# Chunked attention on one core: the softmax scaling moved from GpSimd to ScalarE, TensorE held to the lanes' order, one entry of the planner's table lowered

## The chip, the core and the metric

One core of a Trainium2 chip runs the whole kernel. Times are device microseconds (us) of one execution; the time before is the median of three runs. Engines are named as in the profile: PE is TensorE (PEld its weight loads), DVE is VectorE, ACT is ScalarE, POOL is GpSimd, SP is SyncE, which issues most DMAs. Each engine takes its instructions in the order in which they stand in its own queue; between engines, semaphores make one wait for another.

## The reference

A trunk of two layers over 1024 positions of width 1024, float32. Layer 0 mixes with two recurrent head groups, layer 1 with chunked softmax attention; each layer then has an MLP of width 4096 and a gated embedding. The change touches only the attention:

```python
CHUNK, C_HEADS, C_HEAD_DIM, C_WINDOW_CHUNKS, C_MAX_REL = 64, 16, 64, 8, 256

def chunk_band_attention(h, w_qkv, q_g, k_g, rel_bias):
    qkv = (h @ w_qkv).reshape(bsz, seq, 3, C_HEADS, C_HEAD_DIM)
    q = rmsnorm(qkv[:, :, 0], q_g) * (C_HEAD_DIM ** -0.5)
    k = rmsnorm(qkv[:, :, 1], k_g)
    v = qkv[:, :, 2]
    ...
    def one_chunk(c):          # a chunk of 64 queries against its own and the previous 8 chunks
        ...
        s = jnp.einsum('bqhd,bkhd->bhqk', q_c, k_b).astype(jnp.float32) + bias
        s = jnp.where(valid, s, -jnp.inf)
        prob = jax.nn.softmax(s, -1).astype(v.dtype)
        return jnp.einsum('bhqk,bkhd->bqhd', prob, v_b)
```

## The kernel before

All large products run on PE in three passes (high times high, high times low, low times high), with each operand split into a rounded part and a rest. Layer 0 and the tails of both layers (output product, MLP, gate) fill most of the time; the attention of layer 1 is a stretch of some 590 us in the middle of the profile.

**Work of the attention.** There are 16 steps: 8 pairs of heads (`pr`) times two halves of the sequence (`hf`), each of 512 queries. `attn_in` makes q, k and v of a step: dense matmuls into the bank `dps` (24 of 128x384 for 128 positions), then ACT copies q and k out (`qk`, L1699), ACT and DVE the two parts of v (`vs`, L1703 and L1704), and POOL squares and DVE sums and normalises q and k (L1711 to L1715). `attn_norm` transposes q and k on PE (`dps` from `qk`) and splits them (`F`, `Ql`, L1737 to L1740).

**A job** is `attn_block`: one step, one head, 256 queries; 64 jobs in all. For each of its two blocks of 128 queries:

- near scores into the PSUM tile `sn` (up to 384 keys, two banks in turn) and, from the fourth block of the sequence on, far scores into `sf` (up to 256 keys, one bank for all jobs);
- DVE adds the bias to the near scores and takes their maximum (L1795, into the SBUF tile `pb`), masks a corner of the far ones (L1802), takes their maximum (L1803) and forms the negative of the larger (L1804, or L1807 where there are no far ones);
- ACT takes the exp of the far and of the near scores with their sums (L1805, L1808; each has a second row that reads the sum);
- DVE adds the two sums (L1810) and takes the reciprocal (L1811);
- POOL multiplies the block's probabilities, 128 to 640 columns, by it (L1812).

Then PE transposes the probabilities of both blocks, 128x128 at a time, into `pt` (two banks), ACT copies each bank into `ptile` (L317) and DVE writes the rest of the split (L318), and PE multiplies with v into `po` (one bank for the two jobs of a head). After the second job of a head ACT and DVE move the output out (L1853, L1854).

**Order.** The order in which the program writes its instructions comes from `run` (L123): generators, called lanes, yield the name of a waiting time, and the planner's clock `self.now` advances by a price for each matmul (L151 to L165). A lane goes on when the clock has passed its yield by the table's entry in `LAT` (L37); other lanes fill the time. Two attention lanes take the jobs in turn; the other two lanes are `attn_norms` and `attn_ins`, and the latter also does the embedding's product and the first part of the output product (`dps` from `act` and `wq`, 128x512). In a job, `attn_block0` is the time after each block's scores, `attn_block1` the additional time before the transposes, `attn_block2` that after each bank of transposes, `attn_block3` that before the products with v.

On top of it the framework's own scheduler (the context is opened with a simulated timeline) orders each engine's queue anew when the program is closed, by its own estimate of when an instruction can start. In the kernel before it does so for all engines, PE among them.

Of the kernel before, what the change touches and what calls it, by code (L numbers as in the profile page):

```python
# [11 lines left out]
AF = mybir.ActivationFunctionType  # L12
ALU = mybir.AluOpType
# [4 lines left out]
P = 128  # L18
# [60 lines left out]
    "gdn_back4": 1.83,  # L79
    "attn_norm0": 0.24,  # L80
    "attn_block0": 0.97,
    "attn_block1": 4.45,
    "attn_block2": 0.43,
    "attn_block3": 0.94,
    "qk": 11.25,
# [19 lines left out]
class Trunk:  # L105
# [1470 lines left out]
    def layer1_in(self):  # L1576
        nc, tc, a = self.nc, self.tc, self.a
        with ExitStack() as es:
            self.psm = es.enter_context(self.pool("psml1", space=PSUM))
            wp = self.wp = es.enter_context(self.pool("l1a", 2))  # L1580
            self.wr = es.enter_context(self.pool("l1wr", 2))
            self.w1 = es.enter_context(self.pool("l1w1"))
            l1 = es.enter_context(self.pool("l1", 2))
            self.sm = es.enter_context(self.pool("sml1", 2))
            self.yd = [[self.dr.tile([P, HB], F32, tag=f"yd{k}{hf}", name="yd") for hf in range(2)] for k in range(NK)]
            rbl = l1.tile([P, 16], F32, tag="rbl", name="rbl", bufs=1)
            nc.sync.dma_start(out=rbl, in_=a["rb_last"].rearrange("(o c) -> o c", o=1).broadcast_to((P, 16)))

            steps = [(pr, hf) for pr in range(8) for hf in range(2)]
            self.st = {}  # L1590

            self.ql = [[pool.tile([P, HB], F32R, tag=tag, name="Ql", bufs=1) for pool, tag in
                        ((self.accp, f"acc{e}"), (l1, f"Ql{e}"))] for e in range(2)]
            jobs = iter([(s, h, b) for s in range(16) for h in range(2) for b in range(2)])
            self.run([self.attn_lane(steps, jobs, l1, rbl) for _ in range(2)] + [self.attn_norms(steps, l1), self.attn_ins(steps, l1)])

    def attn_ins(self, steps, l1):
        kv = {}
# [146 lines left out]
    def attn_block(self, s, pr, hf, h, blk, l1, rbl):  # L1745

        nc, psm, sm = self.nc, self.psm, self.sm
        V, A, G = nc.vector, nc.scalar, nc.gpsimd
# [9 lines left out]
        def score(ps, m, j0, n):  # L1758
            qs = slice((m % 4) * P, (m % 4) * P + P)
            o = 0  # L1760
            while o < n:
                j = j0 + o
                e = min(n - o, 4 - j % 4)
                ks = slice((j % 4) * P, (j % 4 + e) * P)
                k = K[j // 4]
                self.mm(ps[:, o * P:(o + e) * P], Q[:, h, qs], k[:, h, ks], start=True, stop=False)
                self.mm(ps[:, o * P:(o + e) * P], Ql[h][:, qs], k[:, h, ks], start=False, stop=True)
                o += e
# [16 lines left out]
        for m in (m0, m0 + 1):  # L1785
            n0 = max(0, m - 2)
            nn = m - n0 + 1
            f0 = max(0, m - 4)
            nf = n0 - f0
            pn = psm.tile([P, HB], F32, tag="sn", name="sn", bufs=2)  # L1790
            score(pn[:, 0:nn * P], m, n0, nn)
            mx = sm.tile([P, 4], F32, tag="mx", name="mx", bufs=4)
            pb = self.wp.tile([P, 5 * P], F32, tag="pb", name="pb", bufs=4)
            S = pb[:, nf * P:(nf + nn) * P]
            V.tensor_tensor_reduce(S, pn[:, 0:nn * P], toep[:, (3 - nn) * P:], op0=ALU.add, op1=ALU.max,  # L1795
                                   scale=1.0, scalar=NEG, accum_out=mx[:, 0:1])
            l = sm.tile([P, 4], F32, tag="l", name="l", bufs=4)
            if nf:
                pf = psm.tile([P, HB], F32, tag="sf", name="sf")
                score(pf[:, 0:nf * P], m, f0, nf)  # L1800
                if m >= 4:
                    V.memset(pf[64:128, 0:64], NEG)  # L1802
                V.reduce_max(mx[:, 1:2], pf[:, 0:nf * P], axis=AX.X)  # L1803
                V.tensor_scalar(mx[:, 2:3], mx[:, 0:1], mx[:, 1:2], -1.0, op0=ALU.max, op1=ALU.mult)  # L1804
                A.activation(pb[:, 0:nf * P], pf[:, 0:nf * P], AF.Exp, bias=mx[:, 2:3], accum_out=l[:, 1:2])  # L1805
            else:
                V.tensor_scalar(mx[:, 2:3], mx[:, 0:1], -1.0, None, op0=ALU.mult)  # L1807
            A.activation(S, S, AF.Exp, bias=mx[:, 2:3], accum_out=l[:, 0:1])  # L1808
            if nf:
                V.tensor_tensor(l[:, 0:1], l[:, 0:1], l[:, 1:2], op=ALU.add)  # L1810
            V.reciprocal(l[:, 2:3], l[:, 0:1])  # L1811
            G.tensor_scalar(pb[:, 0:(nf + nn) * P], pb[:, 0:(nf + nn) * P], l[:, 2:3], None, op0=ALU.mult)  # L1812
            probs.append((pb, f0))
            yield "attn_block0"
        yield "attn_block1"
# [8 lines left out]
        for b in range(bank + 1):  # L1824
            pt = psm.tile([P, HB], F32, tag="pt", name="pt", bufs=2)
            for j, (bb, o, c0, c1) in place.items():
                if bb != b:
                    continue
                for e in range(2):
                    if c0 <= 128 * e < c1:  # L1830
                        pb, f0 = probs[e]
# [9 lines left out]
        for j, c0, c1 in segs:  # L1841
            b, o, _, _ = place[j]
# [111 lines left out]
```

## Time and profile before

| | |
|---|---|
| median of 3 runs | 3216.32 us (3211.31 to 3222.58) |
| the profiled execution's own time | 3205.53 us |
| its span, first to last instruction | 3203.8 us |
| mean granted clock of TensorE | 0.973 |
| busy: PE, PEld | 3097.6 us (97%), 2563.5 us (80%) |
| busy: DVE, ACT, POOL | 2018.2 us (63%), 1310.9 us (41%), 720.4 us (22%) |
| of POOL's busy time, the scaling L1812 | 193.2 us, 128 instructions, mean 1515 ns |

Busy shares are means over stages with different limits, so the attention has to be read by itself. In rows of grouped instructions stand the line, engine, operation, out<-in with shapes and the count; behind the first bar the busy time in us and the mean ns of one; behind the second the engine's idle time just before them and who ended it. A row of the list of waits has who waited, for whom, the us in total, how often, and the longest. Most matmuls have L161 or L165 as their line, a helper's, and are told apart by their tiles. PEclk and the granted clock are shares of full speed.

### The profile page before, as it was taken

The numbers are of one execution on the slowest core, as the hardware profiler recorded it, in microseconds if no ns is written. First come the engines' busy times: TensorE is split into PE (matmuls) and PEld (weight loads), VectorE is DVE, ScalarE is ACT, GpSimd is POOL, SyncE is SP. The second block draws the span as 40 slices with busy tenths as digits, with TensorE's granted clock in tenths as the row PEclk, the third lists the DMA queues.
The fourth block names the chain that finished last, engine by engine and source line by source line (L and its number), as shares of the span: only waits on it lengthen the run. The fifth ranks groups of instructions, "written<-read, shape, count | busy, mean of one in ns | idle before, by whom it ended". The sixth has DMA issues, their size and how long they took to land.

```text
span 3203.8 us, 46403 instructions
## 1 busy us (share of the span) xinstructions
PE 3097.6 (97%) x17576; PEld 2563.5 (80%) x17576; DVE 2018.2 (63%) x4020; ACT 1310.9 (41%) x2480; POOL 720.4 (22%) x1106
## 2 busy tenths in 40 slices
PE   7999999999999999999999989889899999999999
PEld 5777777777778888888887988888778888888887
DVE  6566675557649666655546666666768666655542
ACT  4333443334327554311223455555646555312121
POOL 6334543344400000000005344444430000000002
PEclk8999899999889999999999999999999999999999
DMA  3321112222336333522214111110155433522213
GB/s 120 95 62 59 47 53 68 63 66 74 132 97 210 135 119 112 188 94 103 92 60 132 46 32 35 51 32 16 69 177 208 146 120 110 186 104 93 103 49 105
DMA packets 144718, 309.61 MB, mean 97 GB/s; under 512 B 40944, under 2 KB 43120, under 8 KB 144496
## 3 DMA queue, kind: packets, MB, share of 16 engines
q1 hardware_dynamic: 126064, 273.10, 25.5%
q10 hardware_dynamic: 18432, 33.56, 2.7%
q8 instruction: 138, 2.26, 0.3%
q14 instruction: 84, 0.69, 0.1%
HBM read 232.16 MB, written 74.45 MB: 96 GB/s over the span
## 4 chain that ended last, share of the span: by engine, by line
PE 88%; DVE 7%; ACT 2%; issue 1%; DMA 1%; POOL 1%; SPq 0%; ACTq 0%; DVEq 0%; POOLq 0%
PE dps L161 71%; PE ch L161 3%; PE iz L161 2%; PE po L161 2%; PE pm L161 2%; PE tp L161 1%; PE pt L165 1%; PE sn L161 1%; PE py L161 1%; DVE ptile L318 1%; PE pp L161 1%; PE sc L161 0%; PE sf L161 0%; PE dps L165 0%; DVE pb L1795 0%
## 5 line engine op out<-in xcount | busy, mean ns | idle before, releaser
L161 PE MATMUL dps<-r,act 128*128 128x512 f32 x3528 | 824.2, 392 | 0.0
L161 PEld LDWEIGHTS dps<-r,act 128*128 128x128 f32 x3528 | 662.1, 188 | 145.7
L161 PE MATMUL dps<-xg,whi 128*128 128x512 f32 x1280 | 434.4, 415 | 10.7 <-ACT xg L320 7.4
L1452 POOL TENSOR_TENSOR pn<-pn,prs 128x512 f32<-128x512 f32 x32 | 45.7, 1430 | 1556.4 <-ACT prs L354 1462.2
L161 PE MATMUL dps<-late,act 128*128 128x512 f32 x1536 | 352.9, 391 | 0.0
L161 PEld LDWEIGHTS dps<-late,act 128*128 128x128 f32 x1536 | 288.5, 188 | 63.1
L161 PE MATMUL dps<-wq,act 128*128 128x384 f32 x1536 | 302.6, 344 | 3.8 <-DVE vs L1704 2.7
L161 PEld LDWEIGHTS dps<-xg,whi 128*128 128x128 f32 x1280 | 246.0, 197 | 72.9 <-issue 10.7
L161 PEld LDWEIGHTS dps<-wq,act 128*128 128x128 f32 x1536 | 265.7, 190 | 8.7 <-DVE vs L1704 4.6
L161 PE MATMUL dps<-xg,wlo 128*128 128x512 f32 x640 | 264.5, 413 | 3.0 <-DVE wlo L277 3.0
L1328 DVE TENSOR_TENSOR late<-late,dps 128x512 f32<-128x512 f32 x224 | 153.0, 685 | 154.0 <-PE dps L161 121.4
L1812 POOL TENSOR_SCALAR pb<-pb,l 128x640 f32<-128x640 f32 (+4 forms) x128 | 193.2, 1515 | 249.5 <-DVE l L1811 129.4
L1427 DVE TENSOR_TENSOR xw<-xw,dps 128x512 f32<-128x512 f32 x192 | 131.4, 685 | 143.9 <-PE dps L161 141.0
L1226 ACT CAST act<-act 128x1024 fp32r<-128x1024 f32 (+1 forms) x99 | 94.7, 964 | 285.1 <-DMA act<-in_w 148.7
L1226 ACT CAST act<-late 128x512 fp32r<-128x512 f32 x210 | 124.6, 619 | 139.9 <-PE dps L161 123.6
L1227 DVE TENSOR_TENSOR act<-late,act 128x512 fp32r<-128x512 f32 x210 | 139.8, 687 | 25.4 <-ACT act L1226 25.3
L161 PEld LDWEIGHTS dps<-xg,wlo 128*128 128x128 f32 x640 | 125.7, 196 | 33.7 <-issue 4.8
L161 PE MATMUL dps<-xw,act 128*128 128x512 f32 x576 | 138.9, 392 | 0.0
L276 ACT CAST whi<-wraw 128x1024 fp32r<-128x1024 f32 x78 | 81.7, 1047 | 124.0 <-PE dps L161 73.7
L161 PE MATMUL po<-ptile,vs 128*128 128x256 f32 (+1 forms) x576 | 109.9, 303 | 18.0 <-DVE ptile L318 7.9
L161 PEld LDWEIGHTS dps<-xw,act 128*128 128x128 f32 x576 | 108.0, 188 | 24.0
L1227 DVE TENSOR_TENSOR act<-act 128x1024 fp32r<-128x1024 f32 (+1 forms) x99 | 109.9, 1114 | 24.7 <-ACT act L1226 24.0
(472 smaller groups left out, 5392.7 us busy)
## 6 DMA issues: line engine op xcount, KB each, us to landing
act<-in_w SPq DMA_DIRECT2D x68, 512.0 KB
hd<-late ACTq DMA_DIRECT2D x128, 256.0 KB
late<-in_w SPq DMA_DIRECT2D x60, 512.0 KB
wraw<-in_w_in SPq DMA_DIRECT2D x56, 512.0 KB
act<-hd SPq DMA_DIRECT2D x56, 512.0 KB
wraw<-in_w_out SPq DMA_DIRECT2D x21, 512.0 KB
wraw<-in_w_qkv SPq DMA_DIRECT2D x21, 512.0 KB
pn<-pnd SPq DMA_DIRECT2D x32, 256.0 KB
```

What stands on the lines that cost most here:

```text
L161: return self.nc.tensor.matmul(out, lhsT, rhs, start=start, stop=stop)
L165: return self.nc.tensor.transpose(out, in_, ident)
L276: nc.scalar.copy(hi, raw)
L318: nc.vector.tensor_tensor(dst[:, 1, sl], src, dst[:, 0, sl].bitcast(F32), op=ALU.subtract)
L1226: A.copy(hi, s)
L1227: V.tensor_tensor(lo, s, hi.bitcast(F32), op=ALU.subtract)
L1328: V.tensor_tensor(r, t, u, op=ALU.add)
L1427: V.tensor_tensor(x[n][:, sl], x[n][:, sl], ps, op=ALU.add)
L1452: G.tensor_tensor(pn, pn, prs[:, sl], op=ALU.mult)
L1812: G.tensor_scalar(pb[:, 0:(nf + nn) * P], pb[:, 0:(nf + nn) * P], l[:, 2:3], None, op0=ALU.mult)
```

## The change

Three edits: the table's entry for `attn_block1`; the attention's lanes run inside a guard that makes the scheduler keep PE's instructions as the lanes write them (the other engines are still reordered); and the scaling of the probabilities is an ACT instruction, a copy with a scale for each partition, in place of POOL's multiplication.

```diff
-    "attn_block1": 4.45,
+    "attn_block1": 3.50,
...
-            self.run([self.attn_lane(steps, jobs, l1, rbl) for _ in range(2)] + [self.attn_norms(steps, l1), self.attn_ins(steps, l1)])
+
+            with tc.manual_schedule(engines={mybir.EngineType.PE}):
+                self.run([self.attn_lane(steps, jobs, l1, rbl) for _ in range(2)] +
+                         [self.attn_norms(steps, l1), self.attn_ins(steps, l1)])
...
-            G.tensor_scalar(pb[:, 0:(nf + nn) * P], pb[:, 0:(nf + nn) * P], l[:, 2:3], None, op0=ALU.mult)
+            A.activation(pb[:, 0:(nf + nn) * P], pb[:, 0:(nf + nn) * P], AF.Copy, scale=l[:, 2:3])
```

Lines behind the second edit move down by 3, so that the scaling is L1815, and the exps L1808 (far) and L1811 (near). The number of matmuls is the same, and PE's queue is the same up to the attention's first dense matmuls.

**First place: from scores to transposes, PE.** The second step, second head, second 256 queries, in the kernel before. `pb_16443` and `pb_16476` are the probabilities of the job's two blocks, `pt` the banks that their transposes go to; `sn_16652` and `sf_16659` are scores of a later job, and `po_16463` are products of the job before:

```order
L161 MATMUL sn_16652<-F1_16397,Ql_15494 128x384
L165 MATMUL pt_16570<-ident_62,pb_16443 128x128
L161 MATMUL po_16463<-ptile_16510,vs_15503 128x128
L161 MATMUL po_16463<-ptile_16510,vs_15660 128x128 x2
L165 MATMUL pt_16585<-ident_62,pb_16443 128x128
L161 MATMUL sf_16659<-F1_16397,F0_16410 128x128
L161 MATMUL sf_16659<-F1_16397,Ql_15494 128x128
L165 MATMUL pt_16570<-ident_62,pb_16476 128x128
L165 MATMUL pt_16570<-ident_62,pb_16443 128x128
L165 MATMUL pt_16570<-ident_62,pb_16476 128x128
L165 MATMUL pt_16585<-ident_62,pb_16476 128x128
L165 MATMUL pt_16585<-ident_62,pb_16443 128x128
```

In the changed kernel the same job's blocks are `pb_16408` and `pb_16449`, and its products go to `po_16425`, as those of the job before do. Its last far score stands 19 rows above this piece, which ends with the first transposes:

```order
L161 MATMUL sn_16516<-F1_16476,F0_16489 128x128
L161 MATMUL sn_16516<-F1_16476,Ql_15494 128x128
L161 MATMUL dps_16384<-wq0_15872,act_15326 128x384
L161 MATMUL dps_16384<-wq1_15873,act_15326 128x384
L161 MATMUL dps_16384<-wq0_15872,act_15326 128x384
L161 MATMUL dps_16384<-wq0_15872,act_15408 128x384
L161 MATMUL dps_16384<-wq1_15873,act_15408 128x384
L161 MATMUL dps_16384<-wq0_15872,act_15408 128x384
L165 MATMUL pt_16533<-ident_62,pb_16408 128x128
L165 MATMUL pt_16533<-ident_62,pb_16449 128x128
L165 MATMUL pt_16533<-ident_62,pb_16408 128x128
L165 MATMUL pt_16533<-ident_62,pb_16449 128x128
```

Transposes of the first block no longer stand alone between products and scores; the four of a bank come together, behind dense matmuls. In the rows between the last far score and the first transpose stand 15 dense matmuls, 12 smaller ones that transpose or score, and the 12 products of the job before.

**Second place: far scores of neighbouring jobs, PE.** The step that begins the second half of a pair of heads. In the kernel before, the near scores of a job's two blocks and the first block's far scores (`sf_18549`) stand close together, and the second block's far scores 43 rows further on:

```order
L161 MATMUL sn_18540<-F1_18069,F0_18521 128x256
L161 MATMUL sf_18549<-F1_18069,F0_18521 128x256
L161 MATMUL sn_18573<-F1_18069,F0_18521 128x128
L161 MATMUL sn_18540<-F1_18069,Ql_15496 128x256
L161 MATMUL sn_18540<-F1_18508,F0_18521 128x128
L161 MATMUL sn_18540<-F1_18508,Ql_15496 128x128
L161 MATMUL sf_18549<-F1_18069,Ql_15496 128x256
L161 MATMUL sn_18573<-F1_18069,Ql_15496 128x128
L161 MATMUL sn_18573<-F1_18508,F0_18521 128x256
L161 MATMUL sn_18573<-F1_18508,Ql_15496 128x256
L165 MATMUL pt_18593<-ident_62,pb_18483 128x128
```

In the changed kernel both lanes are at their scores there at once; `sf_18619` is the third of four far scores and `sf_18640` the fourth, and the first two stand just above:

```order
L161 MATMUL sn_18610<-F1_18105,F0_18534 128x128
L161 MATMUL sn_18610<-F1_18105,Ql_15496 128x128
L161 MATMUL sn_18610<-F1_18513,F0_18534 128x256
L161 MATMUL sn_18610<-F1_18513,Ql_15496 128x256
L161 MATMUL sf_18619<-F1_18105,F0_18534 128x256
L161 MATMUL sf_18619<-F1_18105,Ql_15496 128x256
L161 MATMUL dps_18501<-wq0_18358,act_15408 128x384
L161 MATMUL dps_18501<-wq1_18359,act_15408 128x384
L161 MATMUL dps_18501<-wq0_18358,act_15408 128x384
L161 MATMUL sn_18633<-F1_18513,F0_18534 128x384
L161 MATMUL sn_18633<-F1_18513,Ql_15496 128x384
L161 MATMUL sf_18640<-F1_18105,F0_18534 128x128
```

The far scores of four blocks, which share one bank, now stand within some 25 rows.

**Third place: the exps of such blocks, ACT.** In the kernel before, the exps of two blocks of a job (`pb_17763`, `pb_17823`) with what stands between them:

```order
L1805 ACTIVATE pb_17763,l_17765<-sf_17766,mx_17762 128x256
L1808 ACTIVATE pb_17763,l_17765<-pb_17763,mx_17762 128x384
L1737 ACTIVATE F1_18069<-dps_18064,vecs_60 64x512
L1699 ACTIVATE qk_17867<-dps_18000,rscol_15448 128x256
L1703 ACTIVATE vs_17868<-dps_18000,rscol_15448 128x2x64
L1737 ACTIVATE F1_18069<-dps_18064,vecs_60 64x512
L1805 ACTIVATE pb_17823,l_17825<-sf_17826,mx_17822 128x256
L1808 ACTIVATE pb_17823,l_17825<-pb_17823,mx_17822 128x384
```

In the changed kernel, at the second place:

```order
L1808 ACTIVATE pb_18566,l_18568<-sf_18569,mx_18565 128x256
L1811 ACTIVATE pb_18566,l_18568<-pb_18566,mx_18565 128x384
L1815 ACTIVATE pb_18566<-pb_18566,l_18568 128x640
L1808 ACTIVATE pb_18596,l_18598<-sf_18599,mx_18595 128x256
L1811 ACTIVATE pb_18596,l_18598<-pb_18596,mx_18595 128x384
L1815 ACTIVATE pb_18596<-pb_18596,l_18598 128x640
L1702 ACTIVATE qk_18376<-dps_18501,rscol_15448 128x256
L1706 ACTIVATE vs_18377<-dps_18501,rscol_15448 128x2x64
L1808 ACTIVATE pb_18616,l_18618<-sf_18619,mx_18615 128x256
L1811 ACTIVATE pb_18616,l_18618<-pb_18616,mx_18615 128x384
L1815 ACTIVATE pb_18616<-pb_18616,l_18618 128x640
```

The scaling stands directly behind a block's exps and ahead of the next block's.

## The prediction

> **What bounds the kernel now.** I read the page first: the busy shares, the forty slices and the shares of the chain that ended last.
>
> ```profile
> span 3203.8 us, 46403 instructions
> PE   7999999999999999999999989889899999999999
> POOL 6334543344400000000005344444430000000002
> PEclk8999899999889999999999999999999999999999
> PE 88%; DVE 7%; ACT 2%; issue 1%; DMA 1%; POOL 1%; SPq 0%; ACTq 0%; DVEq 0%; POOLq 0%
> ```
>
> TensorE (PE) is busy nearly everywhere and carries 88% of the chain, so a saving must be idle PE time or time at a lower clock. Slices 23 to 30, where POOL works again, are the attention. The stretch view cuts them out; the two stretches after it are for the clock.
>
> ```profile
> core 0: us, PE busy (x) PEld busy (x) DVE busy (x) ACT busy (x) POOL busy (x), PEclk, DMA share, GB/s
> 1801.00:2389.00 588.00, 532.39 (x3257) 492.19 (x3257) 415.57 (x1308) 344.99 (x852) 260.19 (x196) 0.95 0.17 55
> 1926.70:1937.30 10.60, 8.31 (x58) 8.05 (x56) 10.17 (x34) 5.91 (x16) 4.90 (x3) 1.00 0.50 168
> 1937.30:1947.50 10.20, 9.43 (x38) 8.24 (x38) 4.47 (x19) 4.29 (x14) 7.41 (x7) 0.50 0.00 0
> ```
>
> From the first score to the last product with V, 588 us, PE idles 588 - 532.4 = 55.6 us. At a clock of 0.95 it also loses 5%, 29.4 us. These 85 us are all that the change can win; the rest of the program keeps its PE work. The list of waits of that stretch, and the PE rows of the grouped instructions, say whom PE waits for:
>
> ```profile
> PE pt L165 <- POOL pb L1812: 14.3, 11, 4.7
> PE sf L161 <- ACT pb L1805: 9.7, 10, 2.3
> L161 PE MATMUL po<-ptile,vs 128*128 128x256 f32 (+1 forms) x576 | 109.9, 303 | 18.0 <-DVE ptile L318 7.9 <-ACT ptile L317 7.0 <-DVE mx L1807 1.8
> L165 PE MATMUL pt<-ident,pb 128*128 128x128 f32 x480 | 90.0, 294 | 18.8 <-POOL pb L1812 14.3 <-DVE ptile L318 3.6
> L161 PE MATMUL sf<-F,F 128*128 128x128 f32 (+1 forms) x96 | 27.8, 297 | 10.2 <-ACT pb L1805 9.7
> ```
>
> Transposes (pt) wait 18.8 us, 14.3 of it for the scaling on POOL; products with V (po) 18.0 us, mostly for the two halves of ptile; far scores (sf, one bank for both lanes) 10.2 us, for the exp that empties the bank. The other 55.6 - 47.0 = 8.6 us are scattered. The longest wait in order of time:
>
> ```profile
> 1869.47 0.28 DVE L1811 RECIPROCAL l<-l 128x1 f32<-128x1 f32 x3
> 1869.80 3.37 POOL L1812 TENSOR_SCALAR pb<-pb,l 128x128 f32<-128x128 f32 x3 [3.48 <-DVE l L1811]
> 1873.22 0.48 PE L165 MATMUL pt<-ident,pb 128*128 128x128 f32 x1 [4.73 <-POOL pb L1812]
> ```
>
> Three scalings stand in a row on POOL, and PE, which had put a transpose directly behind a score, waits 4.73 us.
>
> **The scaling, on ACT.** Durations, by form:
>
> ```profile
> L1812 POOL TENSOR_SCALAR pb<-pb,l 128x640 f32<-128x640 f32 x64 | 124.1, 1938 | 147.9 <-DVE l L1811 96.3 <-DVE rsw L262 29.4 <-PE pt L165 5.3
> L317 ACT CAST ptile<-pt 128x512 fp32r<-128x512 f32 x80 | 45.1, 586 | 49.3 <-PE pt L165 48.7
> L1662 ACT CAST wq<-wraw 128x1024 fp32r<-128x1024 f32 x16 | 16.3, 1052 | 5.2 <-DMA wraw<-in_w_qkv 5.1
> L1808 ACT ACTIVATE pb<-pb,mx 128x384 f32<-128x384 f32 x96 | 58.4, 608 | 6.6 <-DVE mx L1807 6.0 <-DVE mx L1795 0.4
> L1808 ACT ACTIVATION_READ_ACCUMULATOR pb<-pb,mx 128x1 f32 x128 | 24.3, 190 | 0.0
> L1805 ACT ACTIVATE pb<-sf,mx 128x256 f32<-128x256 f32 x64 | 30.4, 475 | 59.6 <-DVE mx L1804 38.7 <-POOL toep L1754 6.4 <-DVE nn L264 3.8
> ```
>
> No row has an ACT copy of 640 columns. It lies between 0.586 us (512 columns) and 1.052 us (1024); a straight line gives 0.70, which I take because 640 is nearest to 512. Against 1.94 us on POOL, 1.24 us leave the way to the transposes. Of the 128 scalings 64 are 640 wide, 64 x 0.70 = 45 us; 64 are 128 to 512 wide, at no more than 0.608 us each: at most 39 us. ACT's 345 us become at most 429 of some 560. I cost that at nothing, because ACT idles 243 us there now; the exception is the place below, where the new instruction stands ahead of an exp that PE waits for. POOL keeps the squares and the bias tables; the 6.4 us for which ACT waits for a table (last row) stay.
>
> The rest of the way, on DVE:
>
> ```profile
> L1802 DVE MEMSET sf<- 64x64 f32 x64 | 7.2, 112 | 20.9 <-PE sf L161 20.0
> L1803 DVE TENSOR_REDUCE mx<-sf 128x1 f32<-128x256 f32 x64 | 26.6, 416 | 0.6
> L1804 DVE TENSOR_SCALAR mx<-mx 128x1 f32<-128x1 f32 x80 | 16.6, 207 | 1.0
> L1810 DVE TENSOR_TENSOR l<-l 128x1 f32<-128x1 f32 x80 | 16.0, 200 | 27.5 <-ACT pb L1808 25.9
> L1811 DVE RECIPROCAL l<-l 128x1 f32<-128x1 f32 x128 | 20.2, 160 | 6.3 <-ACT pb L1808 4.3
> L318 DVE TENSOR_TENSOR ptile<-pt,ptile 128x512 fp32r<-128x512 f32 x80 | 53.6, 683 | 30.2 <-ACT ptile L317 29.6
> L161 PE MATMUL dps<-r,act 128*128 128x512 f32 x3528 | 824.2, 392 | 0.0
> ```
>
> From the end of a far score: 0.112 + 0.416 + 0.207 + 0.475 + 0.608 + 0.190 + 0.200 + 0.160 = 2.37 us, then the scaling: 4.31 us on POOL, 3.07 us on ACT, when nobody else is in the queues.
>
> **TensorE in the lanes' order, with 3.50 in the table.** The last row prices PE's own work: 824.2 / 3528 = 0.234 us for 512 columns, 0.456 ns a column. At the first place shown of the order, the transposes of before stand directly behind a far score; in the new order 9856 columns, 4.5 us, lie between that job's last score and its first transpose (counted over the rows between them). That covers 3.07 us with 1.4 us left for a queue. With 4.45 in the table PE would have got there later, nothing else. The 18.8 us of pt go. The products with V now stand in one run behind their transposes with dense matmuls between: nowhere under 1.5 us of PE work, against 0.586 + 0.683 = 1.27 us for the halves of ptile. The 18.0 us of po go. The scattered 8.6 us stay.
>
> What comes: a fixed order cannot step around a busy bank. At the second place four far scores pass through the one sf bank in close order, a place that the order repeats seven times. Each must wait until ACT has done the exp before, and ACT's row (third place) reads exp, exp, scale, exp, exp, scale; each scale waits for DVE's sum and reciprocal. So the exps that empty the bank follow each other every 0.475 + 0.608 + 0.190 + 0.200 + 0.160 + 0.70 = 2.33 us. Between the far scores PE has 2560, 768 and 1920 columns (1.17, 0.35, 0.88 us), and 0.23 us for each score. It waits 0.93 + 1.75 + 1.22 = 3.9 us, seven times 27 us, where 10.2 stand now.
>
> Idle after: 55.6 - 18.8 - 18.0 - 10.2 + 27.3 = 35.9 us, 19.7 less. The clock: the stretch from 1926.7 idles 2.3 us and is followed by 10.2 us at 0.50. I let the lost 29.4 us go with the idle time: 29.4 x 35.9 / 55.6 = 19.0, a gain of 10.4. For the clock, the Trainium skill (TensorE: Matmul & The Clock Gate, Part 1: The HAM clock gate) says that half rate follows an idle window of about 3.4 us. The trace disagrees, since no wait for sf exceeds 2.3 us and the clock halved behind one.
>
> Sum: 19.7 + 10.4 = 30 us. The profiled execution took 3205.5 us (span 3203.8 and 1.7 around it) and would take 3175.5. The median of the runs shown, 3216.3, lies 10.8 us above it, so I forecast 3216.3 - 30 = 3186. With the scaling at 1.052 us the 21 waits in the far scores grow by 0.35 us each: idle 43.3, clock 22.9, gain 19 us, 3197. If instead ACT does the four exps out of step with the scalings, the bank is free after 0.112 + 0.416 + 0.207 + 0.475 = 1.21 us; 0.73 us are left of the 3.9, the idle time is 14 us, the clock's loss 7, and the gain 64 us: 3152.
>
> **Rivals.** *The clock stays up.* Waits as summed, but too short to halve the clock: gain 19.7 + 29.4 = 49 us, 3167. For it: the new waits are at most 1.8 us each, and the long 4.7 us goes. Against: the stretch from 1926.7, and three waits here fall within 7 us. The rule of the Trainium skill quoted above (same page and section) would make this of it; the trace so far speaks against it.
>
> *The waits only move: no change.* DVE has 416 us of work, 74% of 560, in one queue in order. Two subtractions of ptile (0.683 us each) ahead of a block's maximum already eat the 1.4 us of cover at the transposes. If each of the 64 jobs comes 0.47 us late, the 30 us are back: 3216. For it: waits of 25.9 and 29.6 us of DVE for ACT in the rows above. Against: 55.6 us idle now includes just these.
>
> *Slower: ACT's queue stands still.* On POOL the wait for the reciprocal held up nobody; on ACT it holds up everything behind. ACT's 345 + 84 = 429 us leave 159 us of the 588, 1.24 us for each of 128 scalings; above that mean wait ACT alone is longer than the stretch of today. The bare wait is 0.200 + 0.160 = 0.36 us; one subtraction of ptile and one maximum ahead of it on DVE make it 1.46. At 1.36 us the stretch takes 429 + 174 = 603, 15 us more: 3231. For it: in ACT's row nothing stands between exp and scale. Against: over the light steps the queue has room to catch up, and DVE is the less loaded the longer the stretch.
>
> **How the numbers follow.** Forecast (3186, or 3197 with the dear scaling) 0.45; clock stays up 0.10; far scores almost free 0.08; no change 0.16; slower 0.21. A measurement of this kernel tells about 0.3%, 9.6 us, from no change. Faster by more: 0.45 + 0.10 + 0.08 = 0.63; within it 0.16; slower 0.21. The range runs from the case with free scores, 3152, to just short of the slow one, 3229.
>
> **What would show it.** Right: no PE wait for L1815's scaling above some 3 us in total, po's idle time under 5 us, sf's at 20 to 35 us in clumps of three, seven times; ACT at about 75% and the stretch near 558 us at a clock of 0.96 to 0.97. Wrong: transposes that wait for ACT's scaling by tens of us (the slow case), waits of po that remain (DVE late), sf under 10 us (more gain), or another length outside the stretch.

## The result, and the profile after

| | before | changed |
|---|---|---|
| median | 3216.1 us (3211.3 to 3222.6, 4 runs) | 3325.2 us (3323.3 to 3326.5, 4 runs) |
| ratio, 95% interval | | 1.0345 [1.0327, 1.0364] |
| span of the profiled execution | 3203.8 us | 3324.7 us |
| scaling of 640 columns | 1938 ns on POOL | 829 ns on ACT |

The change makes the kernel 3.4% slower; 3186 us were forecast, and 3229 was the upper end. The page of the changed kernel, the lines that answer to those shown of before:

```profile
span 3324.7 us, 46091 instructions
PE   7999999999999999999998888888779999999999
POOL 6343543335200000000042000000020000000002
PEclk8999999999989999999998988888889999999999
PE 83%; DVE 8%; ACT 5%; DMA 2%; issue 1%; POOL 1%; SPq 0%; DVEq 0%; ACTq 0%; POOLq 0%
```

POOL is nearly empty from slice 23 on, as it should be, but PE has fallen to 8 and 7 in slices 22 to 30, and the chain leaves PE for DVE, ACT and a DMA more often. In the stretches view, with a window that holds the attention of both kernels (1801 to 2490 us), the changed kernel:

```profile
core 0: us, PE busy (x) PEld busy (x) DVE busy (x) ACT busy (x) POOL busy (x), PEclk, DMA share, GB/s
1801.00:2490.00 689.00, 557.83 (x3197) 516.18 (x3196) 416.60 (x1303) 423.52 (x979) 66.46 (x69) 0.89 0.13 44
2084.00:2092.00 8.00, 4.41 (x18) 3.69 (x19) 4.32 (x20) 5.33 (x17) 0.00 (x0) 0.65 0.15 48
```

And before, in the same window:

```profile
1801.00:2490.00 689.00, 633.39 (x3693) 574.12 (x3693) 497.26 (x1434) 409.11 (x958) 260.19 (x196) 0.96 0.23 77
```

PE idles 131.2 us where it idled 55.6, 75.6 more; and at 0.89 it loses 11% of 689 us, 75.8, where it lost 4%, 27.6. Together 207 against 83 us, 124 more: the 120.9 us by which the span has grown, within the two decimals of the clock. The pages' totals say the same without the clock: over the whole span PE idles 182.9 us where it idled 106.2, 76.7 more, and is busy 3141.8 us where it was 3097.6, 44.2 more for the same 17576 matmuls. PE got through 3197 matmuls in the window instead of 3693; the dense work that it did not reach is done behind it, at full clock. So the loss lies in the attention and has two parts, 76 us of waits and 48 of clock. The waits of PE there, changed kernel:

```profile
PE sf L161 <- ACT pb L1808: 54.0, 32, 3.2
PE dps L165 <- DVE F L1743: 41.1, 14, 3.7
PE po L161 <- DVE ptile L318: 10.4, 11, 1.8
PE pt L165 <- DVE ptile L318: 5.6, 3, 4.8
PE pt L165 <- ACT pb L1815: 1.1, 1, 1.1
```

The scaling is no longer waited for (1.1 us where it was 14.3 on POOL). The far scores wait 54.0 us for the exp that empties their one bank, 9.7 before. And there is a row that did not exist: transposes into `dps` (L165, those of q and k in `attn_norm`) wait 41.1 us for DVE's F, that is until the transposes of k have been taken out of the bank that those of q want. All the waits of these transposes together, before and in the changed kernel, from 1780 to 2560 us:

```profile
L165 PE MATMUL dps<-ident,qk 128*128 128x128 f32 x128 | 20.4, 277 | 1.5 <-DVE vs L1704 1.2
L165 PE MATMUL dps<-ident,qk 128*128 128x128 f32 x128 | 20.9, 288 | 46.4 <-DVE F L1743 42.8 <-DVE vs L1707 3.2 <-ACT sq L1511 0.4
```

The order of time shows both; first four far scores in a row, PE in the changed kernel:

```profile
2080.76 0.27 PE L161 MATMUL sf<-F,Ql 128*128 128x256 f32 x1
...
2084.39 0.39 PE L161 MATMUL sf<-F,F 128*128 128x256 f32 x1 [2.07 <-ACT pb L1808]
...
2087.31 0.58 PE L161 MATMUL sf<-F,F 128*128 128x256 f32 x1 [1.96 <-ACT pb L1808]
...
2090.95 0.47 PE L161 MATMUL sf<-F,F 128*128 128x128 f32 x1 [1.25 <-ACT pb L1808]
```

Waits of 2.07, 1.96 and 1.25 us, 5.3 us at a place for which the prediction had 3.9, and 4.41 us of work in the 8 us from 2084 (the window above), with the clock at 0.65. Some 20 us on, a far score that the prediction did not count, all engines:

```profile
2106.49 0.68 DVE L318 TENSOR_TENSOR ptile<-pt,ptile 128x512 fp32r<-128x512 f32 x1
2107.55 0.69 DVE L318 TENSOR_TENSOR ptile<-pt,ptile 128x512 fp32r<-128x512 f32 x1
2108.16 0.20 DVE L1807 TENSOR_SCALAR mx<-mx 128x1 f32<-128x1 f32 x1
2108.40 0.47 ACT L1808 ACTIVATE pb<-sf,mx 128x256 f32<-128x256 f32 x1 [1.80 <-DVE mx L1807]
2109.01 0.38 PE L161 MATMUL sf<-F,F 128*128 128x256 f32 x1 [2.59 <-ACT pb L1808]
```

Two subtractions of ptile and another block's bias stand on DVE ahead of the maximum's last step; ACT waits 1.8 us for it, and PE 2.59 us for ACT. And the transposes of k and q, PE in the changed kernel:

```profile
2118.09 0.60 PE L165 MATMUL dps<-ident,qk 128*128 128x128 f32 x4
2118.45 0.77 PE L161 MATMUL dps<-wq,act 128*128 128x384 f32 x3
2119.20 0.41 PE L165 MATMUL pt<-ident,pb 128*128 128x128 f32 x2
2123.00 0.63 PE L165 MATMUL dps<-ident,qk 128*128 128x128 f32 x4 [3.38 <-DVE F L1743]
```

Five matmuls of another kind lie between the two groups of transposes. A dense product still gathers in the other `dps` bank, so the group of q stands still for 3.38 us, and everything behind it too.

### The profile page after: what moved, and what is told of

It reads as the page before. It is cut to its first block, busy times and chain, and to the rows that moved or that the text cites. A ratio compares the mean times of both kernels' runs of the same rounds, so it can differ in the third digit from the quotient of the medians.

```text
span 3324.7 us, 46091 instructions
## 1 busy us (share of the span) xinstructions
PE 3141.8 (94%) x17576; PEld 2602.3 (78%) x17576; DVE 2023.0 (61%) x4020; ACT 1391.3 (42%) x2608; POOL 525.3 (16%) x978
## 4 chain that ended last, share of the span: by engine, by line
PE 83%; DVE 8%; ACT 5%; DMA 2%; issue 1%; POOL 1%; SPq 0%; DVEq 0%; ACTq 0%; POOLq 0%
PE dps L161 66%; PE ch L161 3%; PE po L161 2%; PE iz L161 2%; PE pm L161 2%; PE tp L161 1%; PE py L161 1%; PE pt L165 1%; DMA wraw<-in_w_qkv 1%; PE sn L161 1%; ACT pb L1815 1%; DVE pb L1798 1%; PE sf L161 1%; ACT pb L1808 1%; DVE ptile L318 1%
## 5 line engine op out<-in xcount | busy, mean ns | idle before, releaser
L161 PE MATMUL dps<-wq,act 128*128 128x384 f32 x1536 | 343.3, 371 | 2.1 <-DVE vs L1707 0.8
L161 PEld LDWEIGHTS dps<-wq,act 128*128 128x128 f32 x1536 | 290.8, 209 | 3.5 <-ACT late L1449 1.1
L277 DVE TENSOR_TENSOR wlo<-wraw,whi 128x1024 fp32r<-128x1024 f32 x78 | 101.1, 1297 | 28.6 <-ACT whi L276 28.4
L1332 ACT ACTIVATE late<-late 128x512 f32<-128x512 f32 x128 | 80.1, 628 | 80.7 <-DVE late L1328 73.3
```

The lines of the kernel that those rows point to most:

```text
L161: return self.nc.tensor.matmul(out, lhsT, rhs, start=start, stop=stop)
L277: nc.vector.tensor_tensor(lo, raw, hi.bitcast(F32), op=ALU.subtract)
L1332: A.activation(t, t, AF.Relu)
```

## The experiments

Theory A: TensorE's fixed order costs, since PE then stands before a busy bank and cannot step past it. Theory B, the slower rival of the prediction: the scaling in ACT's queue costs. Theory C: the entry 3.50 crowds the lanes by itself. The three edits were taken apart first. The scheduler too has done its work before the program runs; "scheduler" and "lanes" in the table say who wrote PE's queue. No run holds PE to the scheduler's own order, so what is tested is the order that the lanes write, and not the guard by itself.

| scaling | PE's order | entry 4.45 | entry 3.50 |
|---|---|---|---|
| POOL | scheduler | 1 (before) | not run |
| ACT | scheduler | 0.9960 [0.9945, 0.9975] | 0.9967 [0.9953, 0.9982] |
| POOL | lanes | 1.0217 [1.0200, 1.0234] | 1.0377 [1.0347, 1.0407] |
| ACT | lanes | 1.0213 [1.0198, 1.0228] | 1.0345 [1.0327, 1.0364] |

Each ratio in this part is against runs of the kernel before on the same chip, whose medians lie between 3207.4 and 3211.5 us, lower than the 3216.1 beside the changed kernel; differences between kernels of different chips are therefore good to some 9 us only.

**The scaling on ACT alone.**

```diff
-            G.tensor_scalar(pb[:, 0:(nf + nn) * P], pb[:, 0:(nf + nn) * P], l[:, 2:3], None, op0=ALU.mult)
+            A.activation(pb[:, 0:(nf + nn) * P], pb[:, 0:(nf + nn) * P], AF.Copy, scale=l[:, 2:3])
```

> The scaling on ACT alone, with the scheduler free on all engines and 4.45 in the table. Theory A (TensorE's fixed order costs: it stands before a busy PSUM bank and cannot step past it): the waits of pt for the scaling, 14.3 us, go, and nothing takes their place; 3185 to 3220 us against 3216. Theory B (the scaling in ACT's queue costs: it waits for DVE's reciprocal and holds up the exps behind it): most of the 109 us are there without the fixed order too, 3280 us or more.

Measured: 3195.0 us, 0.9960 [0.9945, 0.9975]. Its PE waits and its stretch:

```profile
PE po L161 <- DVE ptile L318: 7.5, 11, 1.6
PE pt L165 <- ACT pb L1812: 7.1, 9, 1.8
PE sf L161 <- ACT pb L1805: 2.9, 7, 0.7
1801.00:2490.00 689.00, 644.46 (x3763) 581.86 (x3762) 501.65 (x1451) 488.53 (x1096) 69.81 (x68) 0.98 0.24 80
```

Theory B falls: with 80 us more on ACT the kernel is 0.4% faster, PE waits less for the exps (2.9 us at sf instead of 9.7), and the waits for the scaling are halved. No version of the study is faster; it beats both kernels.

**The lanes' order alone.**

```diff
+            with tc.manual_schedule(engines={mybir.EngineType.PE}):
+                self.run([self.attn_lane(steps, jobs, l1, rbl) for _ in range(2)] +
+                         [self.attn_norms(steps, l1), self.attn_ins(steps, l1)])
```

> TensorE in the lanes' order alone, the scaling on POOL, 4.45 in the table. Theory A: the waits of sf for the exps (54 us after the change) and of the transposes of q and k for their bank (46 us) are there with POOL as well; 3290 to 3360 us, with a clock of about 0.90 in the attention. Theory B: within 20 us of 3216.

Measured: 3276.0 us, 1.0217 [1.0200, 1.0234]. PE's waits in it:

```profile
PE sf L161 <- ACT pb L1808: 30.3, 28, 4.0
PE dps L165 <- DVE F L1743: 29.2, 12, 3.4
PE dps L161 <- DVE vs L1707: 12.5, 6, 2.8
```

Both waits of Theory A are there with the scaling on POOL. The time lies 14 us under the range of Theory A, with a clock of 0.94 in the attention where 0.90 was expected, and three times as far from before as Theory B allowed: the mechanism holds, its size at 4.45 was put too high.

**Order and scaling, 4.45 kept.** The first two diffs together.

> The changed kernel with 4.45 in the table again. If the lowered entry matters little, as the 7 us that pt waits after the change suggest: within 15 us of 3325. If the earlier transposes are what crowds the queues: 3290 or less.

Measured: 3277.3 us, 1.0213 [1.0198, 1.0228]. The second expected case: under a fixed order the lowered entry costs 48 us (3277.3 to 3325.2; 42 by the two ratios). PE's waits:

```profile
PE sf L161 <- ACT pb L1808: 28.3, 28, 3.9
PE dps L165 <- DVE F L1743: 27.5, 12, 3.2
```

Against these, the changed kernel waits 26 us more at sf and 14 us more at the transposes.

**Scaling and 3.50, the scheduler free.**

```diff
-    "attn_block1": 4.45,
+    "attn_block1": 3.50,
-            G.tensor_scalar(pb[:, 0:(nf + nn) * P], pb[:, 0:(nf + nn) * P], l[:, 2:3], None, op0=ALU.mult)
+            A.activation(pb[:, 0:(nf + nn) * P], pb[:, 0:(nf + nn) * P], AF.Copy, scale=l[:, 2:3])
```

> The scaling on ACT and 3.50 in the table, the scheduler free on all engines. Theory A (only the fixed order costs): as with the scaling alone, 3180 to 3210 us. Theory C (3.50 itself crowds the attention's lanes, in whatever order TensorE runs): 3230 us or more.

Measured: 3199.8 us, 0.9967 [0.9953, 0.9982], no different from the scaling alone. Theory C falls: without the fixed order the entry does nothing that can be measured.

**Order and 3.50, the scaling on POOL.**

```diff
-    "attn_block1": 4.45,
+    "attn_block1": 3.50,
...
+            with tc.manual_schedule(engines={mybir.EngineType.PE}):
```

> TensorE in the lanes' order and 3.50 in the table, the scaling on POOL. If the 48 us between 4.45 and 3.50 (3277 and 3325 us, both with the scaling on ACT) come from PE's order alone, they are here too: 3310 to 3345. If they need the scaling in ACT's queue (Theory B in a smaller form): 3290 or less.

Measured: 3330.5 us, 1.0377 [1.0347, 1.0407]. The 50 us of the entry need no scaling on ACT. Of the whole loss, then, the fixed order makes some 66 us (3276.0 against 3209.6 beside it) and the entry under it some 50; the scaling takes 13 off when the order is free, and nothing that can be told from zero with it at 4.45. At 3.50 the intervals with the scaling on POOL and on ACT overlap too, though PE waits 38.8 us at sf in this kernel and 54.0 in the changed one.

**The planner told of both banks.** The next kernels keep the changed kernel's computation and ask whether the two waits are the cause or only where lateness shows. Before a far score the lane yields until 2.6 us have passed since the last one, and `attn_norm0` is raised:

```diff
-    "attn_norm0": 0.24,
+    "attn_norm0": 3.50,
...
+                while self.now < self.sf_free:
+                    self.lat["sf"] = self.sf_free - self.now
+                    yield "sf"
                 pf = psm.tile([P, HB], F32, tag="sf", name="sf")
                 score(pf[:, 0:nf * P], m, f0, nf)
+                self.sf_free = self.now + 2.60
```

> The changed kernel, and the planner told of the two banks: it keeps 2.6 us from one far score to the next far score of any lane, and 3.50 in place of 0.24 from the transposes of k to those of q. No computation is changed, only the lanes' order. Theory A: waits of sf fall from 54 to under 15 us, those of the transposes of q and k from 46 to under 12, the clock in the attention rises to 0.95 or more, and the time falls by 90 to 140 us, to 3185 to 3235. Theory B: the exps are as late as before, other waits take the place, and the time stays above 3290.

Measured: 3275.3 us, 1.0203 [1.0186, 1.0221]. PE's waits:

```profile
PE pt L165 <- ACT pb L1820: 28.6, 13, 5.3
PE pt L165 <- DVE ptile L318: 12.5, 13, 2.7
PE sf L161 <- ACT pb L1813: 8.4, 6, 2.5
```

The time lies between the two expected ranges. Half of Theory A: sf's waits fall to 8.4 us and those of the transposes of q and k to 2.0, 50 us come back and the clock rises to 0.93, but transposes of probabilities now wait 28.6 us for the scaling. Moving some rows moves all, and the fixed order finds another late instruction.

**Only the transposes of k and q spaced.**

```diff
-    "attn_norm0": 0.24,
+    "attn_norm0": 3.50,
```

> The changed kernel with 3.50 in place of 0.24 from the transposes of k to those of q; only the lanes' order changes. Theory A: the 46 us that these transposes wait for their bank fall under 10, sf's 54 us stay, the time falls by 40 to 70 us, to 3255 to 3285. If these waits only stand for other lateness that is then met elsewhere: less than 20 us.

Measured: 3287.2 us, 1.0244 [1.0220, 1.0269]; 38 us under the changed kernel (32 by the ratios), short of the 40 expected. PE's waits:

```profile
PE sf L161 <- ACT pb L1808: 51.2, 34, 3.6
PE dps L161 <- DVE vs L1707: 23.0, 14, 2.7
```

The wait removed is gone (1.9 us), sf's stays, and a new one, of dense products for the bank that `vs` empties, takes 23 us.

**The same with 4.45.** The edit before, and `attn_block1` at 4.45.

> The changed kernel with 4.45 in the table again and 3.50 from the transposes of k to those of q. Theory A: the 35 us of waits of the transposes of q and k go, the 28 us of sf stay; 3225 to 3250 us against 3277 without the second edit. If other waits take their place, as they did where both banks were spaced out: 3260 or more.

Measured: 3271.5 us, 1.0198 [1.0175, 1.0221]; 6 us under 3277.3, which the intervals don't separate. The case "other waits take their place": sf's rose from 28 to 40 us, and the transposes of probabilities from 6 to 18.

**Only the far scores spaced.** The `sf_free` lines above, in the changed kernel.

> The changed kernel, and the planner keeps 2.6 us from one far score to the next of any lane; the rest as changed. If the neighbouring far scores are what 3.50 adds to a fixed order (sf 28 us of waits with 4.45, 54 with 3.50, and a clock of 0.89 behind them): sf under 20 us and 3270 to 3290 us, the time with 4.45. If the 50 us of 3.50 sit elsewhere: above 3300.

Measured: 3250.8 us, 1.0126 [1.0103, 1.0150]. PE's waits and stretch:

```profile
PE dps L165 <- DVE F L1744: 43.3, 14, 3.5
PE sf L161 <- ACT pb L1813: 9.3, 8, 1.7
1801.00:2490.00 689.00, 600.97 (x3550) 551.35 (x3549) 467.37 (x1377) 464.34 (x1039) 67.99 (x69) 0.94 0.20 66
```

74 us come back (70 by the ratios), 20 more than expected at best. sf's waits fall by 45 us and the clock rises from 0.89 to 0.94, worth 34 us; the wait of the transposes is untouched. So with the entry at 3.50 the crowded far scores carry most of the change's loss: their own waits, and the clock behind them.

**Order, scaling, 4.45, both banks spaced.**

```diff
-    "attn_norm0": 0.24,
+    "attn_norm0": 3.50,
...
+                while self.now < self.sf_free:
...
-    "attn_block1": 3.50,
+    "attn_block1": 4.45,
```

> TensorE in the lanes' order, the scaling on ACT, 4.45 in the table, both banks spaced in the planner (2.6 us between far scores, 3.50 between the transposes of k and q). If a planner that knows the two banks suffices for a fixed order: 3215 to 3240 us. If each wait removed is met again at the next matmul, because no table of constant times knows when DVE and ACT are late: 3255 to 3285, as with either spacing alone.

Measured: 3235.7 us, 1.0078 [1.0052, 1.0103], in the first expected range: the best fixed order of the study, still slower than the scheduler's with the same scaling, 1.0078 against 0.9960, by 38 us. PE's longest waits and its stretch:

```profile
PE dps L161 <- DVE vs L1708: 16.2, 16, 2.5
PE po L161 <- DVE ptile L318: 11.3, 14, 2.1
PE pt L165 <- DVE ptile L318: 11.1, 6, 4.2
1801.00:2490.00 689.00, 613.30 (x3597) 556.31 (x3596) 479.23 (x1394) 470.03 (x1055) 67.32 (x69) 0.95 0.21 70
```

No single wait stands out any more; what is left is spread.

**Only the far scores spaced, 4.45.**

```diff
+                while self.now < self.sf_free:
...
-    "attn_block1": 3.50,
+    "attn_block1": 4.45,
```

> TensorE in the lanes' order, the scaling on ACT, 4.45 in the table, far scores spaced by 2.6 us in the planner. If the far scores are the larger part of the loss at 4.45 too: 3235 to 3255 us against 3277, and then 3.50 costs nothing by itself (3251 with it). If at 4.45 they were far enough apart already (1.7 us and more): 3265 to 3280, and 3.50 with spacing is the better entry.

Measured: 3286.6 us, 1.0244 [1.0227, 1.0261]. The second case, a little above its range: at 4.45 spacing gains nothing, though sf's waits fall from 28.3 to 6.1 us. Its transposes of q and k wait 43.7 us (1790 to 2500 us), and its clock is 0.91. With the far scores spaced, 3.50 is the better entry by 36 us, so 3.50 is not bad in itself; it was bad with four far scores in a row.

**The scheduler free, the planner spaced.** Two kernels, with the scaling on ACT: both spacings, and the far scores alone, with the diffs above.

> The scaling on ACT with the scheduler free, and both banks spaced in the planner, whose order is then only the scheduler's starting point. If that order guides the scheduler: 3170 to 3190 us against 3195 with the scaling alone. If the scheduler's own timeline decides: 3190 to 3205.

> The scaling on ACT with the scheduler free, and only the far scores spaced in the planner. With sf at 3.5 us of waits in the scaling alone there is little to win: 3185 to 3205 us.

Measured: 3202.9 us, 0.9974 [0.9959, 0.9989], and 3204.1 us, 0.9979 [0.9967, 0.9991]. Neither beats the scaling alone. Where the scheduler is free, spacing the lanes' order gains nothing that can be measured, just as the entry of 3.50, which crowds the far scores under the lanes' order, costs nothing (3199.8 us above).

## Why the prediction was wrong

**What bounds the kernel: right.** The loss is idle PE time and clock in the attention; nothing else of the span changed by more than the dense work that moved behind the window.

**The scaling: right, its size off.** 829 ns against 700 taken (829 lies inside the bounds 586 and 1052). "I cost that at nothing" held, and alone it gains 13 us. But it did not take the whole 14.3 us of waits: 7.1 stay, with the scheduler free.

**The 18.8 us of pt and the 18.0 us of po: partly.** In the changed kernel pt idles 7.3 us and po 15.8. The cover between scores and transposes was real. For po I compared PE's work with the bare 1.27 us of the two halves; the list of waits shows 10.4 us for ptile's second half, which stands in DVE's queue.

**The far scores: the mechanism right, the size half.** 27.3 us predicted, 54.0 measured. The seven clumps of three waits are there. At the place that I worked out, 5.3 us instead of 3.9: the waits were 2.07, 1.96 and 1.25 us where I had 0.93, 1.75 and 1.22. Ahead of the first exp DVE took the near scores' bias, the mask and the maximum one after the other, and I had let the exps follow each other without them. The seven clumps together wait 35 us. Most of the rest, 17.5 us, is one more wait some 20 us behind each clump, as at 2109 us, where DVE's queue makes the exp late; the prediction has none of these.

**"The scattered 8.6 us stay": wrong, and the step that failed first.** I carried over the waits that the trace of before showed and gave them new sizes. The transposes of q and k idled 1.5 us before, because the scheduler put other matmuls there: 11 to 25 between the two groups in all but one of the 16 steps. In the lanes' order, where the planner leaves 0.24 us between the two groups, 3 to 7 matmuls stand there, and the transposes idle 46.4 us. The order showed the rows; I looked for places of the waits that I knew.

**The clock: the sign wrong.** I let its loss fall with the idle time, from 29.4 to 19.0 us; it rose to 75.8. The proportion was not even the error: 29.4 x 131.2 / 55.6 is 69, close to what came. The idle time was wrong.

**"With 4.45 in the table PE would have got there later, nothing else": wrong.** Under a fixed order the entry sets the whole order, 48 us' worth, and by way of other rows than those it names: both lanes reach their scores at once.

**The rivals.** The slower one had the right side and the wrong mechanism: PE waits 1.1 us for the scaling, and the kernel is as slow with the scaling on POOL (3276 and 3330 us, against 3277 and 3325). The scaling does delay exps in the clumps. Before the second far score with a wait shown above, DVE had the exp's maximum ready at 2086.47 us, and ACT began the exp behind the scaling:

```profile
2085.98 0.83 ACT L1815 ACTIVATE pb<-pb,l 128x640 f32<-128x640 f32 x1 [1.04 <-DVE l L1814]
2086.71 0.46 ACT L1808 ACTIVATE pb<-sf,mx 128x256 f32<-128x256 f32 x1
```

That is part of what sf waits, but the time is no shorter without it. The clock did not stay up. Not settled: whether holding PE to a fixed order costs anything when the order is a good one, and why a fixed order with both banks spaced still loses 38 us to the scheduler's; its waits are spread over seven rows of 5 to 16.2 us, and no run took them apart.

## What to carry to other kernels

When an order is frozen, every shared buffer that the old order stepped around can become a wait: go through all the banks and their reuse in the new order, not through the waits in the old profile, which shows only what the scheduler could not avoid. Test the parts of a joint change apart: here one of three gains 0.4%, and the other two cost 3.8%. Price a clump of waits with the clock behind it; here the waits were 76 us and the clock 48.

## What the runs showed of the hardware

Waits of 2 us are enough to lower the clock. The first row is the kernel before, directly ahead of the 10.2 us at 0.50 that the prediction shows; the other two are the changed kernel, ahead of a fall and behind it:

```profile
1933.90:1937.30 3.40, 1.11 (x11) 0.92 (x9) 3.39 (x10) 1.50 (x5) 3.01 (x2) 1.00 0.41 147
2083.00:2086.40 3.40, 0.97 (x6) 0.76 (x6) 3.12 (x13) 1.58 (x5) 0.00 (x0) 1.00 0.18 69
2086.40:2096.60 10.20, 8.04 (x26) 7.54 (x27) 3.20 (x16) 6.77 (x18) 1.39 (x2) 0.50 0.09 24
```

Ahead of the falls PE was busy for 1.11 and 0.97 of 3.4 us, with one wait of 2.29 us in the first place, and in the second parts of the two waits of 2.07 and 1.96 us shown above. The Trainium skill (TensorE: Matmul & The Clock Gate, Part 1: The HAM clock gate) puts the fall behind an idle window of about 3.4 us; the runs here show it without a wait that long. How busy PE must be to keep the clock, no run here measures. Spacing the far scores brought the clock from 0.89 to 0.94 together with 43 us less idle time.

ACT's scaled copy from SBUF takes longer than its copies out of PSUM would suggest: 829 ns for 640 columns, and 716 for 512, where the cast of 512 columns out of `pt` took 586 before. The two differ in the scale and the output's type as well, so the reason is not shown. The rows in the changed kernel:

```profile
L1815 ACT ACTIVATE pb<-pb,l 128x640 f32<-128x640 f32 x64 | 53.0, 829 | 23.9 <-DVE l L1814 23.3 <-ACT ptile L317 0.3
L1815 ACT ACTIVATE pb<-pb,l 128x512 f32<-128x512 f32 x16 | 11.5, 716 | 1.6 <-DVE l L1814 1.5
```
